# A two-layer decoder trunk: the first normalisation transposed ahead of its scale and offset

## The chip, the cores and the metric

The kernel runs on one core of one Trainium2 chip. The metric is device time in microseconds of one execution of the whole program; lower is better. TensorE (PE in the profile) multiplies and transposes, VectorE (DVE) and ScalarE (ACT) work on elements, GpSimd (POOL) does elementwise work and issues DMAs, SyncE (SP) issues DMAs.

## What is computed

Two post-norm layers on 256 tokens of 2048 channels. Each has a token mixer with cross-attention, an output projection, a first layer norm, a product-key expert retrieval (PEER) on the normalised tokens, and a second layer norm. What matters here, cut from the reference:

```python
def layer_norm(z, g, b):
    mu = jnp.mean(zf, axis=-1, keepdims=True)
    var = jnp.mean(jnp.square(zf - mu), axis=-1, keepdims=True)
    return (zf - mu) * lax.rsqrt(var + LN_EPS) * g + b

for i in range(DEPTH):                                   # 2 layers
    ...                                                  # mixer and cross-attention
    mix = jnp.concatenate([local, mem_out], axis=-1) @ w_o[i]
    x = layer_norm(DEEPNORM_ALPHA * x + mix, ln_g[i, 0], ln_b[i, 0])
    ffn = peer_ffn(x, peer_wq[i], peer_keys[i], peer_u[i], peer_v[i])
    x = layer_norm(DEEPNORM_ALPHA * x + ffn, ln_g[i, 1], ln_b[i, 1])
```

`peer_ffn` first multiplies x with `peer_wq` (2048 x 2048) for its queries.

## The kernel before

Tokens lie on partitions as two blocks of 128 (`c` = 0, 1) in `xres` (128 x 2 x 2048). Matmuls contract over channels, so each projection needs its input transposed: `xx` (tiles `xa` for channel blocks 0 to 7, `xb` for 8 to 15), with channels on partitions, each value as a `hi` and a `lo` part whose sum carries float32 precision. `split` (L102, L103) makes such a pair: ScalarE writes `hi`, VectorE subtracts it from the source for `lo`. Weights go the same way: `cut` loads 1 MB from DRAM into one of two `raw` buffers on SP's queue (L138), ScalarE makes `hi` and VectorE `lo` of it, 2048 wide, in two buffers each.

The first normalisation, `norm`, stands between the output projection (L171 to L173, whose results L849 adds to `xres`) and the query projection (`proj_t` with `peer_wq`, `mm_t` at L167 and L168). It takes the statistics (L229 to L235: `mv` the mean and variance, `rs` one over the deviation, `nm` minus mean times `rs`) and then goes through four chunks of 512 channels. In each chunk block 0 is normalised by two VectorE operations with the scale and offset rows of `gbt` (L254, L255), block 1 too in the first chunk; in the other three block 1 goes to ScalarE (L259) and GpSimd (L260 for the scale, L261 for the offset). `put_x` then transposes four 128 x 128 pieces of a block into one of two `tr` banks of PSUM (L271) and splits the bank into `xx`. Afterwards GpSimd's queue stores the normalised `xres` to `x1d` (L869), which is read back after the expert scan. `gbt` is `xres`-shaped data: 512 scales and 512 offsets, the same in every partition, loaded by GpSimd's queue (L249).

The first weight group of the query projection is two blocks of 256 columns. A block has two halves of 8 channel blocks, each one load of 1 MB; of each channel block TensorE makes two pairs of L167 (512 columns) and L168 (256 columns). So the first group has four weight halves: first and second for `xa`, third and fourth for `xb`. Behind the group come single blocks with the scores of the product keys (L443) between them; the `keys` tile is loaded on SP's queue (L422).

Each engine works through its own queue in a fixed order. The framework that builds the program sets that order when the program is built: it moves instructions by when it takes their inputs to be ready, so the order isn't that of the source text. Semaphores guard the dependencies, and an instruction that waits holds up all that stand behind it on its engine. `norm` stands twice in the program, once for each layer.

## Time and profile before

| what | us |
| --- | --- |
| median of 3 runs | 3461.08 (3458.07 to 3463.72) |
| profiled execution, its own time | 3457.87 |
| span of the profiled execution | 3456.1 |
| TensorE busy | 3323.3 |
| VectorE busy | 2433.7 |
| ScalarE busy | 1792.3 |
| GpSimd busy | 1317.7 |

The profile is of one execution. The table of engines says who is busy over the whole span; views of a stretch say who is in one place; a timeline lists one engine's instructions in order of time with the idle time before them and what ended it. An instruction is named by its line in the kernel, its operation, and the tiles it writes and reads.

### The profile page before, as it was taken

The page shows a single profiled execution, that of the slowest core. Times are in us where ns is not written, and L with a number is a line of the kernel's source. Part 1 is how long each engine was busy: PE and PEld are TensorE (multiplying, and loading weights), DVE is VectorE, ACT ScalarE, POOL GpSimd, SP SyncE. Part 2 cuts the span into 40 slices and gives each one's busy share as a digit, 9 for nine tenths or more (in the row PEclk, how much of TensorE's full clock was granted, in tenths as well). Part 3 has the DMA queues.
Part 4 walks back from the last instruction along what each step waited for, and adds up shares of the span by engine and source line. Part 5 has one row for each costly group of instructions (what it writes and reads, how often), then busy time and mean ns, then how long its engine had stood idle before and what let it go on. Part 6 is the DMA issues. An engine that isn't in the chain of part 4 may idle for free.

```text
span 3456.1 us, 48912 instructions
## 1 busy us (share of the span) xinstructions
PE 3323.3 (96%) x18444; PEld 2820.3 (82%) x18444; DVE 2433.7 (70%) x3842; ACT 1792.3 (52%) x2404; POOL 1317.7 (38%) x1008
## 2 busy tenths in 40 slices
PE   8998999999999799999999989999999999799997
PEld 7887888888888677877788878888888888688885
DVE  5657788677786477777755767786777785577777
ACT  4433445677744455555444433444777544455554
POOL 0001001587601268886000010001878301488885
PEclk9999999999999899999999999999999999899999
DMA  8454556558796688888554445555478777688885
GB/s 291 153 195 159 193 201 212 187 198 251 232 272 251 213 310 319 320 323 300 186 187 168 161 172 194 201 206 209 176 229 248 234 250 264 230 318 319 320 320 208
DMA packets 242320, 810.39 MB, mean 234 GB/s; under 512 B 120224, under 2 KB 120736, under 8 KB 173728
## 3 DMA queue, kind: packets, MB, share of 16 engines
q1 hardware_dynamic: 176160, 464.83, 40.7%
q0 software_dynamic: 65920, 342.41, 27.2%
q8 instruction: 145, 2.38, 0.3%
q14 instruction: 95, 0.78, 0.1%
HBM read 733.75 MB, written 73.40 MB: 234 GB/s over the span
## 4 chain that ended last, share of the span: by engine, by line
PE 39%; DVE 5%; issue 3%; DMA 2%; ACT 1%; POOL 0%; POOLq 0%; ACTq 0%; DVEq 0%
PE acc L167 13%; PE acc L168 7%; PE acc L172 4%; PE acc L173 4%; PE acc L171 3%; DVE lo L103 2%; DMA raw<-in_u_dram 1%; PE tr L172 1%; PE tr L173 1%; PE g L172 1%; PE g L173 1%; PE tr L171 1%; PE g L171 1%; ACT hi L102 1%; PE g L575 1%
## 5 line engine op out<-in xcount | busy, mean ns | idle before, releaser
L103 DVE TENSOR_TENSOR lo<-raw,hi 128x2048 fp32r<-128x2048 f32 (+1 forms) x520 | 1069.8, 2058 | 422.8 <-ACT hi L102 421.5
L102 ACT CAST hi<-raw 128x2048 fp32r<-128x2048 f32 (+1 forms) x520 | 895.3, 1722 | 452.0 <-PE acc L167 257.5
L167 PE MATMUL acc<-xa,hi 128*128 128x512 f32 x2656 | 958.2, 398 | 3.7 <-ACT hi L102 3.7
L167 PE MATMUL acc<-xb,hi 128*128 128x512 f32 x2656 | 935.4, 390 | 0.0
L168 PE MATMUL acc<-xa,lo 128*128 128x256 f32 x2656 | 758.5, 286 | 16.3 <-DVE lo L103 15.6
L168 PE MATMUL acc<-xb,lo 128*128 128x256 f32 x2656 | 750.6, 283 | 0.0
L167 PEld LDWEIGHTS acc<-xa,hi 128*128 128x128 f32 x2656 | 501.7, 189 | 102.9 <-ACT hi L102 4.4
L167 PEld LDWEIGHTS acc<-xb,hi 128*128 128x128 f32 x2656 | 498.7, 188 | 103.6
L694 POOL DMA_DIRECT2D agd<-am x256 | 143.3, 560 | 1066.5 <-ACT am L693 1043.4
L168 PEld LDWEIGHTS acc<-xa,lo 128*128 128x128 f32 x2656 | 504.7, 190 | 27.2 <-DVE lo L103 25.8
L168 PEld LDWEIGHTS acc<-xb,lo 128*128 128x128 f32 x2656 | 501.9, 189 | 0.7 <-DVE lo L103 0.3
L552 POOL TENSOR_SCALAR eq<-iota_n,nidx1T,sT 128x128 bf16<-128x128 bf16 x256 | 425.2, 1664 | 82.5 <-PE tr L577 76.4
L756 POOL DMA_INDIRECT ag<-agd,iw x226 | 352.3, 1559 | 86.0 <-issue 77.4
L103 DVE TENSOR_TENSOR lo<-vr,hi 128x2048 fp32r<-128x2048 f32 x114 | 261.1, 2290 | 79.8 <-ACT hi L102 78.7
L102 ACT CAST wh<-w 128x128 fp32r<-128x128 f32 (+1 forms) x226 | 78.9, 349 | 457.0 <-PE g L172 380.9
L693 ACT ACTIVATE am<-am 128x256 f32<-128x256 f32 x256 | 107.2, 419 | 389.4 <-DVE am L178 389.3
L557 DVE SCALAR_TENSOR_TENSOR pc<-iota_b,idx2T,gT 128x256 f16<-128x256 bf16 x512 | 221.6, 486 | 116.0 <-PE tr L577 116.0
L172 PE MATMUL acc<-lo,wh 128*128 128x512 f32 x664 | 268.2, 404 | 3.9 <-DVE lo L103 3.9
L173 PE MATMUL acc<-hi,wl 128*128 128x512 f32 x664 | 261.6, 394 | 1.7 <-DVE wl L103 1.7
L171 PE MATMUL acc<-hi,wh 128*128 128x512 f32 x664 | 208.4, 392 | 33.2 <-ACT wh L102 33.2
L743 POOL DMA_INDIRECT vr<-in_v_dram,iv x114 | 191.7, 1682 | 80.9 <-DVE lo L103 38.4
L102 ACT CAST hi<-vr 128x2048 fp32r<-128x2048 f32 x114 | 217.8, 1911 | 2.5 <-PE g L173 1.4
(258 smaller groups left out, 4745.9 us busy)
## 6 DMA issues: line engine op xcount, KB each, us to landing
raw<-in_u_dram SPq DMA_DIRECT2D x256, 1024.0 KB, 5.1
raw<-in_peer_wq_dram SPq DMA_DIRECT2D x32, 1024.0 KB, 4.8
agd<-am POOLq DMA_DIRECT2D x256, 128.0 KB, 4.5
raw<-in_w_in_b_dram SPq DMA_DIRECT2D x56, 512.0 KB, 4.0
agd<-gt SPq DMA_DIRECT2D x64, 320.0 KB, 7.8
rh<-in_w_in_a_dram SPq DMA_DIRECT2D x32, 512.0 KB, 4.3
rh<-in_w_o_dram SPq DMA_DIRECT2D x32, 512.0 KB, 3.7
raw<-in_w_o_dram SPq DMA_DIRECT2D x32, 512.0 KB, 4.1
```

The costliest lines, as they stand in the source:

```text
L102: nc.scalar.copy(hi, src)
L103: nc.vector.tensor_tensor(lo, src, hi.bitcast(F32), op=ALU.subtract)
L167: nc.tensor.matmul(o, wh, x1.rearrange("p n a t -> p (n a t)"), start=dc == 0, stop=False)
L168: nc.tensor.matmul(o[:, :T], wl, x1[:, 0, 0, :], start=False, stop=dc == ND - 1)
L171: nc.tensor.matmul(o, sh, mh, start=first, stop=False)
L172: nc.tensor.matmul(o, sh, ml, start=False, stop=False)
L173: nc.tensor.matmul(o, sl, mh, start=False, stop=last)
L552: nc.gpsimd.tensor_scalar(eq1[:, t, :], iota_n, n1, sc, op0=ALU.is_equal, op1=ALU.mult)
L557: nc.vector.scalar_tensor_tensor(pc[:, t], iota_b[:, None, :].to_broadcast([P, 2, NB]), idx["i2"][:, k:k + 1], idx["g"][:, k, :, None].to_ ...
L694: nc.gpsimd.dma_start(out=a3[:, b, :T], in_=am)
L743: nc.gpsimd.indirect_dma_start(out=vr, out_offset=None, in_=a[f"v{layer}"], in_offset=bass.IndirectOffsetOnAxis(ap=box["iv"][:, k:k + 1], ...
L756: nc.gpsimd.indirect_dma_start(out=ag, out_offset=None, in_=agd[:, :], in_offset=bass.IndirectOffsetOnAxis(ap=box["iw"][:, k:k + 1], axis=0))
```

## The change

`norm` is rewritten, and it gets the scales and offsets a second time in another layout: `gbT`, 128 x 32 values, with a channel in each partition (16 columns of scales, 16 of offsets), loaded by GpSimd's queue.

```diff
-    def norm(y, xo, stats, eps, gb, after):
+    def norm(y, stats, eps, gb, gbT, after):
         r = [ln_rstd(stats, c, eps) for c in range(NC)]
         xx = new_x()
         for ch in range(4):
-            gbt = gb(ch)
-            affine(y, xo, r[0], 0, ch, gbt, False)
-            affine(y, xo, r[1], 1, ch, gbt, ch != 0)
-            for c in range(NC):
-                put_x(xo, xx, c, ch)
+            f = slice(ch * 512, ch * 512 + 512)
+            nc.scalar.activation(y[:, 1, f], y[:, 1, f], AF.Identity, scale=r[1][1], bias=r[1][2])
+            nc.vector.tensor_scalar(y[:, 0, f], y[:, 0, f], r[0][0][:, 0:1], r[0][1], op0=ALU.subtract, op1=ALU.mult)
+            for h in range(2):
+                pt = tr_bank()
+                for j in range(2):
+                    dc = 4 * ch + 2 * h + j
+                    zt = pt[:, j * T:j * T + T]
+                    for c in range(NC):
+                        nc.tensor.transpose(zt[:, c * P:c * P + P], y[:, c, dc * P:dc * P + P], ident)
+                for j in range(2):
+                    dc = 4 * ch + 2 * h + j
+                    zt, x1 = pt[:, j * T:j * T + T], xx(dc)[:, 0]
+                    g, b = gbT[:, dc:dc + 1], gbT[:, ND + dc:ND + dc + 1]
+                    nc.scalar.activation(x1[:, 0, :], zt, AF.Identity, scale=g, bias=b)
+                    t = sm.tile([P, T], F32, name="xt", tag="cr", bufs=3)
+                    nc.vector.tensor_scalar(t, zt, g, b, op0=ALU.mult, op1=ALU.add)
+                    nc.vector.tensor_tensor(x1[:, 1, :], t, x1[:, 0, :].bitcast(F32), op=ALU.subtract)
             after(ch)
+        for ch in range(4):
+            f, gbt = slice(ch * 512, ch * 512 + 512), gb(ch)
+            for c, eng in ((1, nc.gpsimd), (0, nc.vector)):
+                eng.tensor_tensor(y[:, c, f], y[:, c, f], gbt[:, :512], op=ALU.mult)
+                eng.tensor_tensor(y[:, c, f], y[:, c, f], gbt[:, 512:], op=ALU.add)
         return xx
...
         gbl = [load_gb(lnp, 2 * layer, ch, 4) for ch in range(4)]
+        gbT = lnp.tile([P, 2 * ND], F32, name="gbT")
+        nc.gpsimd.dma_start(out=gbT, in_=a["ln_gbT"][layer])
...
-        xx = norm(xres, xres, stats, eps, gbl.__getitem__, after)
+        xx = norm(xres, stats, eps, gbl.__getitem__, gbT, after)
...
+        "ln_gbT": np.concatenate([z[:, 0].reshape(L, ND, P).transpose(0, 2, 1) for z in (ln_g, ln_b)], axis=2),
```

Now only mean and deviation are applied ahead of the transposition (L280 on ScalarE for block 1, L281 on VectorE for block 0). A `tr` bank takes half a chunk: two channel blocks with both token blocks (L288). Scale and offset, now one value for each partition, are applied on the way out of PSUM: by ScalarE into `hi` (L293), by VectorE into a float32 tile `xt` (L295), from which VectorE subtracts `hi` for `lo` (L296). `xres` in its natural layout gets scale and offset (L301, L302) in place, block 1 on GpSimd and block 0 on VectorE, once the chunk has been transposed; it is needed for the store to `x1d`. GpSimd does so for four chunks instead of three.

The build gives another order around `norm`; it is the same in both layers, and the rest of the program keeps its order but for some places in the key search just behind. On VectorE, from the statistics on, before:

```order
L103 TENSOR_TENSOR lo<-raw,hi 128x2048
L233 RECIPROCAL rs<-sd 128x1
L229 BN_AGGR mv<-stats 128x2
L254 SCALAR_TENSOR_TENSOR xres<-xres,mv,gbt 128x512
L235 SCALAR_TENSOR_TENSOR nm<-mv,rs 128x1
L233 RECIPROCAL rs<-sd 128x1
L255 SCALAR_TENSOR_TENSOR xres<-xres,rs,gbt 128x512
```

and in the changed kernel:

```order
L103 TENSOR_TENSOR lo<-raw,hi 128x2048
L233 RECIPROCAL rs<-sd 128x1
L229 BN_AGGR mv<-stats 128x2
L103 TENSOR_TENSOR lo<-raw,hi 128x2048
L235 SCALAR_TENSOR_TENSOR nm<-mv,rs 128x1
L233 RECIPROCAL rs<-sd 128x1
L281 TENSOR_SCALAR xres<-xres,mv,rs 128x512
L235 SCALAR_TENSOR_TENSOR nm<-mv,rs 128x1
L281 TENSOR_SCALAR xres<-xres,mv,rs 128x512 x3
L301 TENSOR_TENSOR xres<-xres,gbt 128x512
L295 TENSOR_SCALAR xt<-tr,gbT 128x256
```

The second weight half (`lo<-raw,hi`) has moved from behind the third chunk's L254 to the front, and the first L301 stands ahead of the first L295. Further on VectorE, up to the third and fourth weight halves, before:

```order
L254 SCALAR_TENSOR_TENSOR xres<-xres,mv,gbt 128x512
L103 TENSOR_TENSOR lo<-raw,hi 128x2048
L103 TENSOR_TENSOR xb<-tr,xb 128x4x128 x2
L255 SCALAR_TENSOR_TENSOR xres<-xres,rs,gbt 128x512
L103 TENSOR_TENSOR lo<-raw,hi 128x2048
L103 TENSOR_TENSOR xb<-tr,xb 128x4x128 x2
L103 TENSOR_TENSOR lo<-raw,hi 128x2048
```

and in the changed kernel:

```order
L301 TENSOR_TENSOR xres<-xres,gbt 128x512 x2
L295 TENSOR_SCALAR xt<-tr,gbT 128x256 x2
L296 TENSOR_TENSOR xb<-xt,xb 128x256 x2
L295 TENSOR_SCALAR xt<-tr,gbT 128x256
L302 TENSOR_TENSOR xres<-xres,gbt 128x512
L296 TENSOR_TENSOR xb<-xt,xb 128x256
L302 TENSOR_TENSOR xres<-xres,gbt 128x512
L301 TENSOR_TENSOR xres<-xres,gbt 128x512
L103 TENSOR_TENSOR lo<-raw,hi 128x2048
L302 TENSOR_TENSOR xres<-xres,gbt 128x512
L103 TENSOR_TENSOR lo<-raw,hi 128x2048
```

All sixteen L295 and L296 and seven of the eight L301 and L302 of block 0 now stand ahead of the third weight half. On TensorE, at the first transpositions and the first matmuls of the query projection (numbers tell buffers apart), before:

```order
L271 MATMUL tr_2222<-ident_72,xres_507 128x128 x4
L271 MATMUL tr_2229<-ident_72,xres_507 128x128 x4
L271 MATMUL tr_2241<-ident_72,xres_507 128x128 x4
L271 MATMUL tr_2248<-ident_72,xres_507 128x128 x4
L167 MATMUL acc_2332<-xa_2216,hi_2276 128x512
L168 MATMUL acc_2332<-xa_2216,lo_2277 128x256
L167 MATMUL acc_2333<-xa_2216,hi_2276 128x512
```

and in the changed kernel:

```order
L288 MATMUL tr_2222<-ident_72,xres_507 128x128 x3
L288 MATMUL tr_2235<-ident_72,xres_507 128x128 x3
L167 MATMUL acc_2387<-xa_2218,hi_2306 128x512
L168 MATMUL acc_2387<-xa_2218,lo_2307 128x256
L167 MATMUL acc_2388<-xa_2218,hi_2306 128x512
L168 MATMUL acc_2388<-xa_2218,lo_2307 128x256
L167 MATMUL acc_2389<-xa_2218,hi_2340 128x512
L288 MATMUL tr_2250<-ident_72,xres_507 128x128 x4
```

Where sixteen transpositions (two chunks) stood ahead of the first matmul, now eight do (one chunk, two halves), and the third half stands behind five matmuls, one of them of the second weight half. On SP's queue `keys` goes from behind the fourth load of `peer_wq` to behind the fifth, and waits for the last L302 of both engines.

## Rows read from the trace of the kernel before

**Rows 1.** The page's table of engines: busy us (share), instructions.

```profile
PE 3323.3 (96%) x18444; PEld 2820.3 (82%) x18444; DVE 2433.7 (70%) x3842; ACT 1792.3 (52%) x2404; POOL 1317.7 (38%) x1008
```

**Rows 2.** Stretches: us, busy PE, PEld, DVE, ACT, POOL; PE clock, DMA share, GB/s.

```profile
267.00:273.00 6.00, 0.06 (x2) 0.02 (x1) 5.98 (x14) 4.19 (x4) 0.00 (x0) 0.88 0.14 22
273.00:281.00 8.00, 4.23 (x17) 3.06 (x18) 7.85 (x9) 3.88 (x6) 6.91 (x5) 0.50 0.28 115
285.20:290.00 4.80, 4.80 (x32) 4.29 (x31) 2.80 (x4) 0.69 (x2) 0.55 (x1) 0.99 0.99 348
320.00:340.00 20.00, 16.69 (x97) 14.37 (x96) 19.97 (x56) 6.67 (x7) 0.00 (x0) 1.00 0.41 158
2058.50:2072.70 14.20, 10.20 (x44) 8.47 (x45) 14.05 (x16) 5.64 (x9) 9.82 (x7) 0.58 0.32 128
```

**Rows 3.** TensorE's timeline, layer 0: start, us, instruction [idle before <-who ended it].

```profile
272.98 1.12 PE L271 MATMUL tr<-ident,xres 128*128 128x128 f32 x4 [5.94 <-DVE xres L255]
276.05 1.11 PE L271 MATMUL tr<-ident,xres 128*128 128x128 f32 x4 [1.95 <-DVE xres L255]
...
281.62 0.63 PE L167 MATMUL acc<-xa,hi 128*128 128x512 f32 x1
282.05 0.41 PE L168 MATMUL acc<-xa,lo 128*128 128x256 f32 x1
...
295.85 0.39 PE L167 MATMUL acc<-xb,hi 128*128 128x512 f32 x1
...
306.94 1.67 PE L443 MATMUL tr<-keys,qT 128*128 128x128 f32 x12
```

**Rows 4.** VectorE's timeline, layer 0.

```profile
269.04 2.26 DVE L103 TENSOR_TENSOR lo<-raw,hi 128x2048 fp32r<-128x2048 f32 x1
271.22 0.16 DVE L233 RECIPROCAL rs<-sd 128x1 f32<-128x1 f32 x1
...
272.19 0.73 DVE L255 SCALAR_TENSOR_TENSOR xres<-xres,rs,gbt 128x512 f32<-128x512 f32 x1
...
274.24 3.44 DVE L255 SCALAR_TENSOR_TENSOR xres<-xres,rs,gbt 128x512 f32<-128x512 f32 x2
...
278.20 1.15 DVE L254 SCALAR_TENSOR_TENSOR xres<-xres,mv,gbt 128x512 f32<-128x512 f32 x1
279.27 0.68 DVE L103 TENSOR_TENSOR xa<-tr,xa 128x512 fp32r<-128x512 f32 x1
...
282.79 1.16 DVE L254 SCALAR_TENSOR_TENSOR xres<-xres,mv,gbt 128x512 f32<-128x512 f32 x1
...
291.49 2.29 DVE L103 TENSOR_TENSOR lo<-raw,hi 128x2048 fp32r<-128x2048 f32 x1 [3.49 <-ACT hi L102]
```

**Rows 5.** GpSimd's timeline, layer 0.

```profile
277.09 1.71 POOL L260 TENSOR_TENSOR xres<-xres,gbt 128x512 f32<-128x512 f32 x1
278.88 1.60 POOL L261 TENSOR_TENSOR xres<-xres,gbt 128x512 f32<-128x512 f32 x1
...
281.79 1.60 POOL L261 TENSOR_TENSOR xres<-xres,gbt 128x512 f32<-128x512 f32 x1
```

**Rows 6.** Groups by line and shape: busy us, mean ns of one | idle before.

```profile
L700 DVE TENSOR_TENSOR w<-ag 128x256 f32<-128x256 f32 x104 | 44.3, 426 | 27.1 <-DMA ag<-agd,iw 23.8
L406 DVE TENSOR_SCALAR sc<-sc,dw 128x256 f32<-128x256 f32 x12 | 3.5, 350 | 0.1
L406 DVE TENSOR_SCALAR sc<-sc,dw 128x128 f32<-128x128 f32 x12 | 2.7, 283 | 0.1
L589 DVE TENSOR_SCALAR m<-tr 128x256 f32<-128x256 f32 x2 | 0.8, 424 | 6.4 <-PE tr L577 6.4
L259 ACT ACTIVATE xres<-xres,nm,rs 128x512 f32<-128x512 f32 x8 | 6.3, 809 | 3.6 <-DVE nm L235 3.6
```

**Rows 7.** SP's queue, layer 0.

```profile
288.13 0.33 SPq L422 DMA_DIRECT2D keys<-in_keysT_dram  x1
293.81 46.78 SPq L138 DMA_DIRECT2D raw<-in_peer_wq_dram  x8
```

## The prediction

> **What bounds the kernel now.** I read the page's table of engines first: TensorE is busy 96% of the span [rows 1], so a change of a normalisation counts only by what TensorE idles or crawls around it. The two first normalisations (one in each layer) are such places. I then read the stretches of layer 0: TensorE does next to nothing from 267 to 273 us and is busy for 4.23 of the next 8 us, at a granted clock of 0.50 (1.2 GHz) after that pause; from 285.2 on it is busy all the time, at 0.99 (2.4 GHz) [rows 2]. TensorE's own timeline gives the marks [rows 3]: first four transpositions at 272.98 after 5.94 us idle, second half of the first weight group (first `xb` matmul) at 295.85, end of the group (the scores' first matmuls) at 306.94. Between the last two marks lie 32 pairs of L167 and L168: (306.94 - 295.85) / 32 = 0.347 us a pair.
>
> Who releases TensorE there is VectorE, busy for 5.98 of 6 us and 7.85 of 8 [rows 2]. Two things are to be seen in its timeline. First, the third weight half (`lo` at 291.49, done at 293.78) comes 2.1 us before TensorE wants it, after 3.49 us idle: VectorE has some 5 us of slack, no more. Second, L254 and L255 are slow beside GpSimd. GpSimd's op of 277.09 ends at 278.80, and the L254 issued at 278.20 ends 0.55 later; GpSimd's op of 281.79 ends at 283.39, and the L254 issued at 282.79 ends 0.56 later; the two L255 of 274.24 take 3.44 together, against 0.73 for the one of 272.19 ahead of GpSimd's first op [rows 4, 5]. So a VectorE operation with two SBUF tensors waits out a GpSimd operation and then runs. The `lo` part of `put_x`, with one tensor in PSUM, keeps its 0.68 in the middle of the GpSimd op of 278.88 [rows 4, 5].
>
> **The change, term by term, for one layer.** The ten L254/L255 and eight 512-wide `xa`/`xb` subtractions go from VectorE. It gets 4 L281, 16 L295, 16 L296 and 8 L301/L302, and in the order seven of those last eight stand ahead of the third weight half.
>
> Start. The second weight half (as the first: 2.26 long, the next start 2.18 after its own [rows 4]) now stands ahead of `nm`, so the first L281 starts near 273.8, where the first L254 followed the first half directly. L281 512 wide: a TENSOR_SCALAR costs 283 ns at 128 and 350 at 256 [rows 6], 67 per 128 elements, so an estimate of 0.48. ScalarE's L280 for the other token block takes 0.81 (L259 [rows 6]) from 274.4, and the eight transpositions of the first chunk end near 276.75 at 0.26 each (1.11 and 1.12 for four, with the last one's latency, at the low clock [rows 3]). Before, the second four ended at 277.2, so this is no loss. But VectorE's next instruction is an L301 that overwrites what is being transposed; it waits, about 1.2 us.
>
> VectorE's work to the third `lo`. L295 reads PSUM: 424 ns, as L589 [rows 6], 0.34 to the next start (0.08 overlaps, as 2.26 against 2.18 above). L296: 426 as L700 [rows 6], 0.34 too. L301/L302: 0.68, 0.61 to the next start. 16 x 0.34 + 16 x 0.34 + 7 x 0.61 + 2.2 for the `lo` = 17.4. From 276.75 that ends at 294.1, even if nothing waits: the same place as before, and all the slack is used.
>
> GpSimd's lock. L296, L301 and L302 have two SBUF tensors each; 23 of them meet 8 GpSimd operations instead of six. Before, the four blocked ones shown lost 3.44 - 1.46 = 2.0 and twice 0.45, or 2.9 us [rows 4]. No row shows a TENSOR_TENSOR with both tensors in SBUF beside a GpSimd operation. Its bounds are the unblocked `xa` subtraction (0) and the blocked L255 (1.0 each). I take the blocked end, since the operands are alike. A GpSimd op runs 1.1 to 1.2 us of its own (that of 278.88 took 1.60, of which it waited for the L254 until 279.35), and VectorE's pairs L296, L296 fall into each: laid beside each other, five are blocked for the whole op (1.15) and three for 0.45 to 0.8, together 7.6 us.
>
> TensorE's order. Only two `tr` banks exist and a bank now holds half a chunk. The third half's transpositions stand behind five matmuls of the first two channel blocks, which wait for L296 of these; L295 of the third half waits for them in turn. At the low clock the next start comes 0.43 after a L167's (281.62 to 282.05 [rows 3]) and half of that after a L168's: 3 x 0.43 + 2 x 0.21 + 4 x 0.26 = 2.75, of which VectorE covers 0.85 with two L296 and a L295 of its own. That makes 1.9 once, and a few tenths at the four later halves: 2.6.
>
> So the third `lo` ends at 294.1 + 7.6 + 2.6 = 304.3, and TensorE, which wanted it at 295.85, gets it 8.5 late. With the short waits at the second one I take **9 us**. ScalarE is no bound: 16 L293 of 0.4 and 4 L280 lie in VectorE's shadow; if it were to wait, each of its waits is one of VectorE's.
>
> Weight loads behind. Two `raw` buffers: a load is issued when an earlier `lo` is done (293.81 against the end at 293.78 [rows 4, 7]). The fifth load moves from 293.8 to 304.4. `keys` on SP's queue now waits for the last L302 and GpSimd's last op, so it is issued at about 305 instead of 288.13 [rows 7], with the sixth load behind it on the queue, and the second store to `x1d`, later on GpSimd's queue because eight ops stand ahead, at 305 too. Four transfers of 1 MB then start within 3 us; at the 348 GB/s of the stretch 285.2 to 290 [rows 2] they need 12 us. So the sixth load lands near 319, its `lo` ends near 323.5 and frees the buffer for the eighth, which lands near 329, where TensorE needs it already cut; the wait there is about 5.7. In before TensorE idles 20 - 16.69 = 3.3 us between 320 and 340 [rows 2], part of which it replaces. Net **3 us**, with 0 and 5 as bounds. The scores wait for `keys` at about 316, inside the same loss. The store is read back only after the expert scan, and `gbT`, 16 KB, is loaded ahead of the last projection block: both cost nothing.
>
> Sum for one layer: 9 + 3 = 12. Layer 1 has the same order and the same picture (14.2 us with 10.20 busy at a clock of 0.58 [rows 2]), so 24. The stages behind are bound by TensorE and carry the delay to the end. The profiled execution took 3457.87, 1.8 over its span, and so 3481.9 after; the median of the three runs stands 3.2 higher, so **3485 us**, 0.7% slower.
>
> In the Trainium skill, the page "SBUF — State Buffer", section "Who interferes with whom", says that a VectorE instruction with two SBUF inputs, `tensor_tensor` included, contends with a GpSimd instruction that reads SBUF, and that the later one blocks fully. The L254 rows agree for their kind of instruction; no row here shows it for a TENSOR_TENSOR. By that rule the lock term is the 7.6 above; if it did not hold for this kind, the term is nought and the sum is the second rival's.
>
> **Rivals.**
> 1. *The start gets shorter and wins.* Transposed values need no scale rows, and per-partition scalars are cheap; TensorE lost 5.94 + (8 - 4.23) = 9.7 us to gaps before 281 [rows 2, 3]. If neither lock nor TensorE's order made VectorE wait, and L295/L296 went at half their rows, 5.4 us less would bring the third `lo` to 288.7, and TensorE, full from 285 now, could be so from about 281.5: 3.5 us a layer, 3485 - 24 - 7 = 3454. It decides from the point at which the third `lo` ends before 295.85. Against it: 17.4 us of work have 19.1 to lie in. Chance 0.05.
> 2. *TENSOR_TENSOR is not blocked by GpSimd.* Then 7.6 falls away, the third `lo` ends at 296.7, 1 to 2 us late with the wait at the fourth, and the bunched loads keep their 3: 5 a layer, 3471. Chance 0.13.
> 3. *Off the path.* The group's later weights have slack enough and TensorE's old idle of 3.3 us at 320 to 340 swallows the delay: 3461 within 0.2%. Against it: 3.3 is less than 9. Chance 0.05.
> 4. *The clock stays at 1.2 GHz longer*, since matmuls now come in short bursts until 300. A pair at that level costs some 0.64 from start to start (0.43 + 0.21 as above) against 0.347; ten more such pairs are 3 us a layer: 3491. Chance 0.10.
>
> **How the numbers follow.** The forecast has 0.67. All but rivals 1 and 3 are slower by more than 0.2% (6.9 us, about what a measurement here can tell from none): 0.90; same 0.05, faster 0.05. The range takes in the bounds of the lock (3471, less 1) and of the clock (3491, plus 1): 3470 to 3492.
>
> **What would show it.** Right: in both layers the third `lo` ends near 304, L296 rows split into 0.42 and 1.2 to 1.6, TensorE's first `xb` pairs come 8 us later and a wait of 4 to 6 us for `lo` stands near 330. Wrong: L296 at 0.42 throughout beside GpSimd (rival 2), first `xb` pairs by 296 (rivals 1, 3), clock under 0.7 to 295 (rival 4). The forecast falls if transpositions of the third half start before 279, since then VectorE is fed early.

## The result: 3484 us, 0.7% slower

The changed kernel took 3484.4 us (median of 4 runs, 3481.9 to 3485.3) beside 3460.6 for the kernel before: a ratio of 1.0066, interval 1.0054 to 1.0079. Five more runs of it beside another set of runs of before (below) gave 3481.4, a ratio of 1.0062, 1.0049 to 1.0076. So it is slower, by 21 to 24 us, where 24 were forecast.

The profile after, read in the order of the prediction. First the table of engines (busy us, share, instructions), which answers to [rows 1]:

```profile
PE 3335.5 (96%) x18444; PEld 2827.8 (81%) x18444; DVE 2454.6 (70%) x3894; ACT 1801.4 (52%) x2422; POOL 1279.9 (37%) x1014
```

The stretches (us, busy PE, PEld, DVE, ACT, POOL; PE clock, DMA share, GB/s), against [rows 2]:

```profile
273.00:281.00 8.00, 2.71 (x9) 1.93 (x10) 7.10 (x14) 4.29 (x7) 3.08 (x2) 0.50 0.60 246
285.20:290.00 4.80, 3.94 (x25) 3.37 (x24) 3.86 (x7) 1.66 (x4) 2.64 (x2) 0.94 0.00 0
304.00:310.00 6.00, 5.81 (x19) 5.04 (x20) 2.94 (x3) 0.00 (x0) 0.55 (x1) 0.52 0.79 239
320.00:340.00 20.00, 17.48 (x93) 15.04 (x92) 20.00 (x84) 5.05 (x6) 0.00 (x0) 0.91 0.46 160
```

TensorE is now idle for 0.86 of the 4.80 us from 285.2 on, where it was full, and no DMA runs there: both `raw` buffers are taken, since no `lo` frees one. From 304 on TensorE runs at half its clock once more, and the transfers that had stood still come together.

TensorE's timeline (start, us, instruction, [idle before <- who ended it]), the marks of [rows 3]:

```profile
274.37 0.69 PE L288 MATMUL tr<-ident,xres 128*128 128x128 f32 x2 [7.27 <-DVE xres L281]
275.29 1.54 PE L288 MATMUL tr<-ident,xres 128*128 128x128 f32 x6 [0.23 <-ACT xres L280]
...
301.10 0.74 PE L167 MATMUL acc<-xb,hi 128*128 128x512 f32 x2 [1.45 <-ACT hi L102]
304.19 0.80 PE L168 MATMUL acc<-xb,lo 128*128 128x256 f32 x2 [2.35 <-DVE lo L103]
...
317.00 2.12 PE L461 MATMUL tr<-keys,qT 128*128 128x128 f32 x16
333.20 0.50 PE L168 MATMUL acc<-xa,lo 128*128 128x256 f32 x2 [2.52 <-DVE lo L103]
```

The first L168 on `xb` stands at 304.19, against 296.08 before: 8.1 late. The first scores stand at 317.00, against 306.94: 10.1 late. From TensorE's timeline before come the first row behind, and the two waits that it had between 320 and 340:

```profile
296.08 0.28 PE L168 MATMUL acc<-xb,lo 128*128 128x256 f32 x1
...
322.27 0.71 PE L443 MATMUL tr<-keys,qT 128*128 128x128 f32 x4 [1.64 <-DVE qT L178]
...
324.66 0.50 PE L168 MATMUL acc<-xa,lo 128*128 128x256 f32 x2 [1.68 <-DVE lo L103]
```

VectorE's timeline and below it GpSimd's, against [rows 4, 5]:

```profile
276.65 0.69 DVE L301 TENSOR_TENSOR xres<-xres,gbt 128x512 f32<-128x512 f32 x1 [0.90 <-PE tr L288]
...
287.18 2.04 DVE L296 TENSOR_TENSOR xa<-xt,xa 128x256 fp32r<-128x256 f32 x2
...
294.50 0.75 DVE L296 TENSOR_TENSOR xb<-xt,xb 128x256 fp32r<-128x256 f32 x2
295.17 1.28 DVE L301 TENSOR_TENSOR xres<-xres,gbt 128x512 f32<-128x512 f32 x2
...
301.85 2.28 DVE L103 TENSOR_TENSOR lo<-raw,hi 128x2048 fp32r<-128x2048 f32 x1
```

```profile
287.58 1.35 POOL L302 TENSOR_TENSOR xres<-xres,gbt 128x512 f32<-128x512 f32 x1
...
295.04 2.57 POOL L301 TENSOR_TENSOR xres<-xres,gbt 128x512 f32<-128x512 f32 x1 [1.65 <-ACT hi L102]
...
299.35 0.59 POOL L889 DMA_DIRECT2D x1d<-xres  x1 [0.30 <-POOL xres L302]
305.03 0.55 POOL L889 DMA_DIRECT2D x1d<-xres  x1 [5.08 <-DVE xres L302]
```

A pair of L296 takes 0.75 where GpSimd is idle, and 2.04 where GpSimd's op of 287.58 starts 0.40 behind it: the first gets through, the second waits out the op. At 295 it is the other way round: GpSimd's op of 295.04 comes while the L296 pair of 294.50 runs and takes 2.57, and VectorE's two L301, which follow that pair at once, run through it at 0.64 each. The third `lo` ends at 304.13.

ScalarE and VectorE at the third half chunk, and further on at the weight half that TensorE waits for near 333:

```profile
283.46 0.56 ACT L293 ACTIVATE xa<-tr,gbT 128x256 fp32r<-128x256 f32 x1 [1.53 <-PE tr L288]
284.06 0.55 DVE L295 TENSOR_SCALAR xt<-tr,gbT 128x256 f32<-128x256 f32 x1 [1.55 <-ACT xa L293]
284.64 0.56 ACT L293 ACTIVATE xa<-tr,gbT 128x256 fp32r<-128x256 f32 x1 [0.62 <-DVE xt L295]
...
324.59 1.92 ACT L102 CAST hi<-raw 128x2048 fp32r<-128x2048 f32 x1 [3.90 <-PE acc L167]
330.87 2.28 DVE L103 TENSOR_TENSOR lo<-raw,hi 128x2048 fp32r<-128x2048 f32 x1
```

L295 reads the bank and not `hi`, and yet it starts only when L293 has ended, and the next L293 when L295 has: in this program the two engines take turns at a bank.

The groups by shape (busy us, mean ns of one | idle before):

```profile
L295 DVE TENSOR_SCALAR xt<-tr,gbT 128x256 f32<-128x256 f32 x32 | 16.4, 537 | 4.3 <-ACT xa L293 4.3
L296 DVE TENSOR_TENSOR xb<-xt,xb 128x256 fp32r<-128x256 f32 x16 | 11.2, 732 | 0.0
L296 DVE TENSOR_TENSOR xa<-xt,xa 128x256 fp32r<-128x256 f32 x16 | 10.8, 708 | 0.0
L302 DVE TENSOR_TENSOR xres<-xres,gbt 128x512 f32<-128x512 f32 x8 | 6.7, 834 | 0.0
```

### The profile page after: what moved, and what is told of

Its sections match the earlier page's. It is cut to its first block, busy times and chain, and to the rows that moved or that the text cites. A ratio compares the mean times of both kernels' runs of the same rounds, so it can differ in the third digit from the quotient of the medians.

```text
span 3483.4 us, 49017 instructions
## 1 busy us (share of the span) xinstructions
PE 3335.5 (96%) x18444; PEld 2827.8 (81%) x18444; DVE 2454.6 (70%) x3894; ACT 1801.4 (52%) x2422; POOL 1279.9 (37%) x1014
## 3 DMA queue, kind: packets, MB, share of 16 engines
q0 software_dynamic: 65984, 342.44, 27.3%
## 4 chain that ended last, share of the span: by engine, by line
PE 39%; DVE 6%; issue 3%; DMA 2%; ACT 1%; POOL 0%; POOLq 0%; ACTq 0%; DVEq 0%
PE acc L167 13%; PE acc L168 7%; PE acc L172 4%; PE acc L173 4%; PE acc L171 3%; DVE lo L103 2%; PE tr L172 1%; PE tr L173 1%; PE g L172 1%; PE g L173 1%; PE tr L171 1%; PE g L171 1%; DMA raw<-in_u_dram 1%; ACT hi L102 1%; PE g L593 1%
## 5 line engine op out<-in xcount | busy, mean ns | idle before, releaser
L167 PE MATMUL acc<-xa,hi 128*128 128x512 f32 x2656 | 965.5, 401 | 10.5 <-DVE xa L296 3.7
L167 PE MATMUL acc<-xb,hi 128*128 128x512 f32 x2656 | 939.4, 392 | 2.9 <-ACT hi L102 2.9
L168 PE MATMUL acc<-xa,lo 128*128 128x256 f32 x2656 | 761.8, 287 | 15.3 <-DVE lo L103 14.3
L168 PE MATMUL acc<-xb,lo 128*128 128x256 f32 x2656 | 752.2, 284 | 4.7 <-DVE lo L103 4.7
L167 PEld LDWEIGHTS acc<-xa,hi 128*128 128x128 f32 x2656 | 505.0, 190 | 111.4 <-issue 8.2
L167 PEld LDWEIGHTS acc<-xb,hi 128*128 128x128 f32 x2656 | 500.6, 189 | 107.8 <-ACT hi L102 3.8
L168 PEld LDWEIGHTS acc<-xa,lo 128*128 128x128 f32 x2656 | 508.3, 192 | 27.2 <-DVE lo L103 25.7
L168 PEld LDWEIGHTS acc<-xb,lo 128*128 128x128 f32 x2656 | 504.1, 190 | 6.4 <-DVE lo L103 5.9
L570 POOL TENSOR_SCALAR eq<-iota_n,nidx1T,sT 128x128 bf16<-128x128 bf16 x256 | 416.4, 1630 | 83.5 <-PE tr L595 77.1
L172 PE MATMUL acc<-lo,wh 128*128 128x512 f32 x664 | 268.0, 404 | 4.6 <-DVE lo L103 4.6
L761 POOL DMA_INDIRECT raw<-in_v_dram,iv x112 | 158.5, 1415 | 119.6 <-DVE lo L103 80.8
```

Source lines behind the costliest of these rows:

```text
L167: nc.tensor.matmul(o, wh, x1.rearrange("p n a t -> p (n a t)"), start=dc == 0, stop=False)
L168: nc.tensor.matmul(o[:, :T], wl, x1[:, 0, 0, :], start=False, stop=dc == ND - 1)
L172: nc.tensor.matmul(o, sh, ml, start=False, stop=False)
L570: nc.gpsimd.tensor_scalar(eq1[:, t, :], iota_n, n1, sc, op0=ALU.is_equal, op1=ALU.mult)
L761: nc.gpsimd.indirect_dma_start(out=vr, out_offset=None, in_=a[f"v{layer}"], in_offset=bass.IndirectOffsetOnAxis(ap=box["iv"][:, k:k + 1], ...
```

## The experiments

The forecast's theory was weighed against three others throughout. It says: VectorE's queue ahead of the third weight half sets the time, with GpSimd's lock in it, and the late `lo` bunches the transfers behind. The others: the lock costs nothing (rival 2), or TensorE's new order of half chunks does it, or the loss isn't about the place ahead of the third half at all.

A table sums up where each kernel stood against the kernel before, by the start of the same instruction in each trace: the first scores of layer 0 (306.94 before), the L172 that waits for `lo` at 1417.68 before, in the stage of the expert values, the first scores of layer 1 (2092.42), and the span's end (3456.1). All in us of delay.

| kernel | scores 0 | 1417.68 | scores 1 | end | median us |
| --- | --- | --- | --- | --- | --- |
| changed kernel | 10.1 | 8.2 | 23.9 | 27.3 | 3484.4 |
| the same, second trace | 10.0 | 10.8 | 20.3 | 21.0 | 3481.4 |
| e1, no GpSimd ops | 3.7 | 5.9 | 10.4 | 15.6 | 3472.4 |
| e2, no VectorE L301/L302 | 4.9 | 8.0 | 11.7 | 11.8 | 3468.3 |
| e3, neither | -0.3 | 1.4 | 1.5 | 4.1 | 3461.9 |
| e4, `xt` on ScalarE | 3.7 | 10.2 | 15.0 | 23.2 | 3482.7 |
| e5, stores held | 9.5 | 7.7 | 18.9 | 19.9 | 3478.3 |
| e6, `keys` early | 9.1 | 13.4 | 25.3 | 29.7 | 3484.8 |
| e7, stores held, no GpSimd ops | 1.7 | 2.5 | 7.2 | 7.9 | 3465.8 |
| e8, moved behind the group | 2.4 | 12.8 | 12.1 | 25.2 | 3482.8 |
| e10, unlocked split | 8.0 | 5.6 | 14.0 | 12.4 | 3470.0 |
| e11, unlocked, stores held | 2.9 | -0.5 | 3.7 | 2.1 | 3459.9 |
| e12, kernel before, stores held | -0.6 | 2.9 | 2.9 | 5.8 | 3460.5 |

The last row shows how far one trace can be trusted: e12 is as fast as the kernel before by its median, and yet its trace is 5.8 late at the end. The stage itself begins at slightly different times too, from 1.3 us earlier (e3) to 1.2 later (e8) than before by the first L229, and that is in the first column. Differences of one or two microseconds in the first column, and of some 3 to 6 in the others, show nothing by themselves; the medians decide.

### Without GpSimd's operations, without VectorE's, without either (e1, e2, e3)

e1's edit; e2 keeps `(1, nc.gpsimd)` alone, and e3 drops the loop (L298 to L302).

```diff
-            for c, eng in ((1, nc.gpsimd), (0, nc.vector)):
+            for c, eng in ((0, nc.vector),):
```

> The scale and offset of the stored copy are left out for token block 1 (the eight GpSimd operations of each layer), so the stored copy of that block is not finished; VectorE's instructions around the normalisation stay the same, in the same order. The forecast's theory: VectorE loses only the time in which it is locked out. In the changed kernel the blocked L296 and the blocked L302 lost 0.62 + 1.07 + 1.29 + 1.25 + 1.31 = 5.5 us in layer 0 against their free 0.75 a pair and 0.65, so all L296 should now show about 0.42, the third `lo` should start at 301.85 - 5.5 = 296.3 and end at 298.6, and with 1 to 1.5 us less from the loads behind it (`keys` and the second store no longer wait for GpSimd) a layer should gain some 6.5 to 7: 3484.4 - 13.5 = 3471 (3467 to 3475). Rival 'the lock hardly matters, it is VectorE's plain work and TensorE's order': 3481 to 3485, with the third `lo` still ending at 303 or later.

Measured: 3472.4 us, ratio to before 1.0031 (1.0021 to 1.0041), 9 to 12 us under the changed kernel's two medians. Its groups (busy us, mean ns of one | idle before), and its third `lo` from VectorE's timeline:

```profile
L296 DVE TENSOR_TENSOR xb<-xt,xb 128x256 fp32r<-128x256 f32 x16 | 6.2, 417 | 0.0
L296 DVE TENSOR_TENSOR xa<-xt,xa 128x256 fp32r<-128x256 f32 x16 | 6.2, 417 | 0.0
L302 DVE TENSOR_TENSOR xres<-xres,gbt 128x512 f32<-128x512 f32 x8 | 5.5, 682 | 0.0
```

```profile
296.60 2.28 DVE L103 TENSOR_TENSOR lo<-raw,hi 128x2048 fp32r<-128x2048 f32 x1
```

VectorE's instructions and their order around the normalisation are the same in both kernels, so the difference of the means is the lock: 16 x (720 - 417) + 4 x (834 - 682) ns = 5.46 us a layer (720 is the mean of 708 and 732). The third `lo` agrees: it ends 22.01 us behind the start of the first L301 (298.88 against 276.87), 27.48 in the changed kernel (304.13 against 276.65), 5.47 less. Rival 2 falls: a TENSOR_TENSOR with both tensors in SBUF is blocked by GpSimd. The 9 to 12 us aren't the lock alone, since the store of block 1 went out earlier too; e7 below sets that right.

> The scale and offset of the stored copy are left out for token block 0 (the eight L301/L302 of VectorE in each layer); GpSimd's eight stay. The order moves: the third `lo` goes ahead of the last two chunks' L295 and L296. The forecast's theory (VectorE's whole queue ahead of the third `lo` sets the time): VectorE loses 4 x (0.68 - 0.07) + 4 x (0.83 - 0.07) = 5.5 us of work with what lock is in it, and the 0.9 us wait of the first L301 for the transpositions; the L296 that are blocked stay blocked. 6.4 a layer, and with the third `lo` ahead of the last chunks 1 to 2 us more from the weight loads: 3484.4 - 2 x 8 = 3468 (3464 to 3473). Rival 'only the lock costs': the lock of the four blocked pairs of L296 (4.9 of 5.5 us) remains, so at most 0.6 a layer: 3483. Rival 'two token blocks' natural copies cost nothing, TensorE's order of half chunks does': 3482 or more.

Measured: 3468.3, ratio 1.0019 (1.0009 to 1.0028). The gain of 13 to 16 us is about what the forecast's theory gave for VectorE's queue (16), and far more than the lock's share in it. VectorE's work is not all of it, though: the third `lo` now stands ahead of the last three L295 (and is itself held up by GpSimd, 3.38 instead of 2.28), and the store of block 0 leaves at 276.59 instead of 305.03, ahead of the bunch. The two rows are from VectorE's and GpSimd's timelines:

```profile
293.53 3.38 DVE L103 TENSOR_TENSOR lo<-raw,hi 128x2048 fp32r<-128x2048 f32 x1
...
276.59 0.54 POOL L889 DMA_DIRECT2D x1d<-xres  x1 [84.21 <-DVE xres L281]
```

> Scale and offset of the stored copy are left out for both token blocks (GpSimd's eight and VectorE's eight operations of each layer, and the loads of their rows). What stays of the change: the half chunks on TensorE, L293, L295 and L296. The forecast's theory: the two removals add, 5.5 of lock and 5.5 + 0.9 of work make 12 us, more than the 9 that TensorE waits in a layer, so the third `lo` ends near 292, TensorE's group ends where it did before (306.9) and the whole goes back to 3460 (3455 to 3465). Rival 'the order of half chunks and the per-partition operations on the way out of PSUM (L295 at 0.54, L296) cost the most': it stays at 3470 or more, with waits of TensorE for `xt` and L296 ahead of the third half. Rival 1 of the prediction (the start gets shorter): 3454 or less.

Measured: 3461.9, ratio 0.9996 (0.9987 to 1.0006). No loss is left that the runs can tell from none, and nothing is gained. The first scores, from TensorE's timeline:

```profile
306.64 1.57 PE L456 MATMUL tr<-keys,qT 128*128 128x128 f32 x12 [0.21 <-DMA keys<-in_keysT_dram]
```

They stand at 306.64, against 306.94 before, in a trace whose stage began 1.3 earlier: a microsecond longer. So the half chunks, L293, L295 and L296 cost about what L254, L255 and `put_x` cost, and nearly the whole loss comes from scale and offset "on the side", with what they do to the stores (which leave at 274.73 and 277.23 here, ahead of the bunch). The gains of e1 and e2, 9 to 12 and 13 to 16, are together as much as the 20 to 23 of e3 or more. Rival 1 falls too: a shorter start isn't there even when the side work costs nothing.

### `xt` on ScalarE (e4)

```diff
-                    nc.scalar.activation(x1[:, 0, :], zt, AF.Identity, scale=g, bias=b)
-                    nc.vector.tensor_scalar(t, zt, g, b, op0=ALU.mult, op1=ALU.add)
+                    nc.scalar.activation(t, zt, AF.Identity, scale=g, bias=b)
+                    nc.scalar.copy(x1[:, 0, :], t)
```

> The whole computation, with another share of it: ScalarE writes `xt` out of PSUM with scale and offset and then copies it to `hi`; VectorE keeps only the subtraction L296. VectorE loses 16 x (0.54 - 0.08) = 7.4 us, ScalarE gets sixteen more operations: 16 x (0.56 + 0.4) + 4 x 0.8 for block 1 + 2 x 1.9 for the weights = 22 us of the 30 us from 274.4 to 304. The forecast's theory (VectorE's queue ahead of the third `lo` is the bound): the third `lo` 6 to 7 us earlier, about as much as the lock allows, and 3484.4 - 2 x 7 = 3470 (3466 to 3476). Rival 'ScalarE, or the longer chain bank, xt, hi, lo, takes the place of VectorE': the group's end moves by 4 us or less, the bunched loads behind it keep their loss, 3480 to 3486.

Measured: 3482.7, ratio 1.0071 (1.0054 to 1.0088): no gain to be measured, and the rival's number, though not for its reason. The first step came in part as the forecast's theory has it: the third `lo` ended at 299.78, 4.4 us earlier than in the changed kernel (6 to 7 were expected), and the first scores came 6.4 earlier. At 1417.68 it was 10.2 late again. Where the gain went is seen in ScalarE's, VectorE's and TensorE's timelines behind the group:

```profile
310.72 1.90 ACT L102 CAST hi<-raw 128x2048 fp32r<-128x2048 f32 x1 [5.11 <-DMA raw<-in_peer_wq_dram]
...
312.65 2.29 DVE L103 TENSOR_TENSOR lo<-raw,hi 128x2048 fp32r<-128x2048 f32 x1 [6.54 <-ACT hi L102]
314.86 0.42 DVE L178 TENSOR_TENSOR qT<-acc,cr 128x256 f32<-128x256 f32 x1
...
315.34 1.65 PE L461 MATMUL tr<-keys,qT 128*128 128x128 f32 x6 [3.92 <-DVE qT L178]
```

Both stores, `keys` and two weight loads are issued from 296.65 on; the fifth weight load, issued at 299.81, is awaited by ScalarE until 310.7. VectorE's `lo` for it waits 6.54 us, the sum for `qT` stands behind it on VectorE's queue, and TensorE's scores wait for that. So the bunch of transfers is a loss of its own.

### The stores, `keys`, and the lock with the stores alike (e5, e6, e7)

e5 holds both stores by adding zero times a column of query block 9 to one column of `xres` ahead of each. e6 gives `keys` a pool of its own (the second diff). e7 is e5 with e1's edit.

```diff
+                z = sm.tile([P, 1], F32, name="z", tag="rs")
+                nc.vector.tensor_scalar_mul(z, qT[:, 9, 0:1], 0.0)
+                for c in range(NC):
+                    nc.gpsimd.tensor_tensor(xres[:, c, 0:1], xres[:, c, 0:1], z, op=ALU.add)
+                    nc.gpsimd.dma_start(out=x1d[c], in_=xres[:, c])
```

```diff
+        kp = right.enter_context(tc.tile_pool(name=f"kp{layer}", bufs=1, side="right"))
...
-        keys = pk.tile([P, 16, P], F32, name="keys")
+        keys = kp.tile([P, 16, P], F32, name="keys")
```

> The whole computation; the two stores to `x1d` are held back until query block 9 (some 340 us): zero times one of its columns is added to one column of `xres` by GpSimd ahead of each store. Around the normalisation nothing else changes. The forecast's theory (its second term): at 304 to 307 us the fifth and sixth weight load, `keys` and the second store start together; without the store three transfers remain, some 3 us less of traffic, the wait of TensorE near 330 shrinks from some 5 us by 2 to 3, and a layer gains 2 to 3: 3484.4 - 5 = 3479 (3476 to 3482). Rival 'the store takes nothing from the loads, only the third `lo` counts': 3484 within 2. Rival 'the bunched transfers are the larger half of the loss': 3474 or less.

Measured: 3478.3, ratio 1.0053 (1.0036 to 1.0069): 3 to 6 us less than the changed kernel's two medians, as the forecast's theory expected in sum, but the intervals overlap, so a gain isn't shown by this run. The place was another, too. The wait for `lo` near 330 went from 2.52 only to 2.17, and the first scores moved by 0.5.

> The whole computation; `keys` gets a pool of its own, whose place in SBUF nothing else uses before it, so that its load no longer waits for the last L302 and stands far ahead on SP's queue. Like the run with the held stores it takes one of four transfers from the bunch at 304 to 307 us, and the sixth weight load no longer stands behind it on the queue. The forecast's theory: a layer gains 1 to 3, 3480 (3477 to 3483); the third `lo` stays at 302. Rival 'the wait near 330 is not for loads': 3484 within 2.

Measured: 3484.8, ratio 1.0071 (1.0053 to 1.0089): nothing gained, the rival's number. Taking `keys` out of the bunch is worth nothing by itself: its trace was ahead by 1 us at the first scores and behind at 1417.68. TensorE's waits near 330 are 1.63 and 1.68 here, as in the kernel before. The prediction had counted `keys` among the causes of its second term.

> As the run with the held stores, and in addition the scale and offset of the stored copy are left out for token block 1 (GpSimd's eight operations of each layer). In the run without GpSimd's operations one of the stores had also moved away from the weight loads, so its gain of 12 us was lock and loads together; here both sides hold their stores alike, and the difference to the run with the held stores is the lock alone. The lock as read from VectorE's rows (5.3 us at the third `lo`: 304.13 against 298.88): 10 to 11 us below that run, 3468 (3465 to 3472). Rival 'the lock's 5.3 us are given back behind the group': within 4 us of it.

Measured: 3465.8, ratio 1.0015 (1.0005 to 1.0024), 12.5 us under e5, with stores alike in both: the lock, 5.46 us a layer by VectorE's rows, comes through to the end with a little more.

### Scale and offset behind the first weight group (e8)

The loop of L298 to L302 and the two stores become a function, called where the first weight group ends; the rows come from the pool of the key search.

```diff
+        gbl = [load_gb(pk, 2 * layer, ch, 4) for ch in range(4)]
...
+            if state["nb"] == 0:
+                natural(xres, gbl.__getitem__, x1d)
```

> The whole computation; the scale and offset of the stored copy (on both engines) and the stores stand behind the first weight group in the program, about 305 us, and their rows are loaded into the pool of the key search. Nothing of it is ahead of the third `lo` any more. Theory 'place': the loss comes from standing ahead of the third and fourth weight half; the group then ends where it did in the run without these operations (306.6), and the whole lands at 3461 to 3467. Rival 'VectorE has no slack behind the group either' (it is busy 19.97 of 20 us from 320 to 340 before the change, 20.00 after): 5.5 us of work and the lock of GpSimd's operations with the 2.2 us `lo` subtractions come back as waits behind 306: 3473 to 3482.

Measured: 3482.8, ratio 1.0064 (1.0047 to 1.0081): just above the rival's range. The first scores were only 2.4 late, in a trace whose stage began 1.2 late, but at 1417.68 it was 12.8. VectorE's and TensorE's rows behind the group:

```profile
309.49 0.69 DVE L304 TENSOR_TENSOR xres<-xres,gbt 128x512 f32<-128x512 f32 x1 [3.43 <-DMA gbt<-in_ln_gb_dram]
...
313.56 3.11 DVE L305 TENSOR_TENSOR xres<-xres,gbt 128x512 f32<-128x512 f32 x2
...
321.85 1.58 DVE L305 TENSOR_TENSOR xres<-xres,gbt 128x512 f32<-128x512 f32 x1
...
328.53 2.29 DVE L103 TENSOR_TENSOR lo<-raw,hi 128x2048 fp32r<-128x2048 f32 x1
...
330.87 0.80 PE L168 MATMUL acc<-xb,lo 128*128 128x256 f32 x2 [5.23 <-DVE lo L103]
```

The same operations, blocked by GpSimd's again (1.4 to 1.8 us each), push the key search back; the `lo` of 328.53 stands behind the key search on VectorE's queue, and TensorE waits 5.2 us for it. The run isn't a clean one, though: the rows are now loaded at this place (2 MB), VectorE waits 3.4 us for the first of them, and they share the DMA with the weights. So it shows that this way of moving the work behind the group gains nothing; how much of the 12.8 is the work and how much the loads stays open.

### The split without two SBUF tensors, and with the stores held (e9, e10, e11, e12)

e9 is the changed kernel once more. e11 is e10 with e5's held stores, and e12 the kernel before with held stores. e10 leaves all work where it is and takes away only what makes L296 wait: the value stays in PSUM.

```diff
-                    nc.vector.tensor_scalar(t, zt, g, b, op0=ALU.mult, op1=ALU.add)
-                    nc.vector.tensor_tensor(x1[:, 1, :], t, x1[:, 0, :].bitcast(F32), op=ALU.subtract)
+                    nc.vector.scalar_tensor_tensor(zt, zt, g, x1[:, 0, :].bitcast(F32), op0=ALU.mult, op1=ALU.subtract)
+                    nc.vector.tensor_scalar(x1[:, 1, :], zt, b, None, op0=ALU.add)
```

> The changed kernel once more, unaltered, for a second trace beside the held stores. In its first trace layer 0 lost 10.1 us up to the first scores, had 8.2 left at 1426 us and then lost 6.6 more in the stage of the expert values (GpSimd's indirect loads of 1532 to 1546 us took 2.4 to 2.8 us to issue instead of 0.95); with the held stores the same stage lost 0.5. If that is chance of one execution, the second trace has 0 to 2 there, a span near 3478, and the median of more rounds comes down to 3479 to 3483. If the early stores cause it, the second trace loses 5 to 7 there again and the median stays at 3484.

Measured: 3481.4 (3478.9 to 3482.4), span 3477.1. In this trace the stage of the expert values lost nothing (10.8 late at 1417.68, 10.8 still at the last statistics of layer 1), so the 6.6 us of the first trace are no property of the change. What made them is open: indirect loads that take over 2 us to issue stand in both traces. The changed kernel's own loss in this trace is 21.0, 10.8 and 10.2 in the two layers.

> The whole computation, written so that VectorE's part of the split has no operation with two SBUF tensors: in place in the PSUM bank it takes scale times the value minus `hi`, and a second operation adds the offset on the way from the bank to `lo`. GpSimd keeps its eight operations, VectorE its eight L301/L302. Forecast's theory (L296 loses 4.9 us a layer to GpSimd's lock): the lock of L296 goes; the second operation now reads PSUM, some 0.1 longer, 1.6 in all; 3.3 us a layer or more are gained, 3477 (3471 to 3480), and no operation of the split shows more than 0.6. Rival 'the bank is held longer, so transpositions wait and eat the gain': 3482 to 3486.

Measured: 3470.0, ratio 1.0033 (1.0023 to 1.0044), 11 to 14 us under the changed kernel, more than expected. The two new operations, with GpSimd as busy beside them as ever:

```profile
L294 DVE SCALAR_TENSOR_TENSOR tr<-tr,gbT,xb 128x256 f32<-128x256 f32 x16 | 7.2, 482 | 0.0
L295 DVE TENSOR_SCALAR xb<-tr,gbT 128x256 fp32r<-128x256 f32 x16 | 7.1, 475 | 0.1
```

```profile
314.96 1.19 PE L460 MATMUL tr<-keys,qT 128*128 128x128 f32 x4 [6.31 <-DMA keys<-in_keysT_dram]
```

The first fence holds groups (mean ns behind the comma), the second is of TensorE's timeline. Neither operation is ever blocked (the longest take 486 and 484 ns). Both together take 0.96 us, against 0.537 + 0.720 = 1.26 for L295 and L296: 16 x 0.30 = 4.8 us a layer. The expectation had 3.3, the lock of L296 less 1.6 for a longer read of PSUM; the second operation is indeed 0.06 longer than a free L296, but the first is 0.055 shorter than L295. The first L168 on `xb` stands at 296.68, 0.6 late instead of 8.1; the order had moved too, the third `lo` (294.35) now stands ahead of the last chunk's operations, and how much of the 11 to 14 that gives isn't shown. What is left is the row of the second fence: TensorE waits 6.3 us for `keys`.

> Both edits, the split without two SBUF tensors and the two stores held until query block 9; the whole computation. If lock and stores are two separate losses, their gains add: 3477 less the 6 that holding gave, 3471 (3463 to 3474), still not below the kernel before (3461), since VectorE's work is longer than before. If both gains are of the same wait, it stays at 3475 to 3478.

Measured: 3459.9, ratio 0.9995 (0.9986 to 1.0005): level with the kernel before, and below both ranges that were expected. The two gains add, 11 to 14 and 10.1, and each is larger than expected. Holding the stores is worth 10 us here, clear of the noise, and 3 to 6 in e5, not clear of it. The DMA view of 300 to 316 us (issues: line, engine, operation, count, KB each, median us to landing) shows why, e10's row first, then e11's:

```profile
keys<-in_keysT_dram SPq DMA_DIRECT2D x1, 1024.0 KB, 9.7
```

```profile
keys<-in_keysT_dram SPq DMA_DIRECT2D x1, 1024.0 KB, 4.9
```

In e10 `keys` is issued at 305.11, right behind the two stores of 303.27 and 304.81, and lands 9.7 us later; in e11 it is issued at 304.81 and lands 4.9 later, and TensorE's wait for it is 1.46 us instead of 6.31.

> A control: the kernel before the change with its two stores held until query block 9, nothing else; the whole computation. If holding the stores only undoes the bunch of transfers that the change makes, it is worth nothing here: 3460, within 4 either way. If it is a gain of its own, whatever the normalisation, it shows here too: 3450 to 3455, and the equality of the unlocked kernel with held stores then hides a remaining loss of the change of 5 to 10 us.

Measured: 3460.5, ratio 1.0001 (0.9992 to 1.0010). Held stores are worth nothing where nothing bunches: what e11 gained by them is loss that the change had made.

No version beat the kernel before. e3 shows why none that keeps this way through the transposition was to be expected: even with the side work left out it takes as long as the old one.

## Why the prediction was right, point by point

The sum came out (3485 forecast, 3484.4 and 3481.4 measured), and so did the first mark: the third `lo` ends at 304.13 in the trace, 304.3 was forecast. The mechanism, VectorE's queue with the lock in it ahead of the third weight half, is the one that the runs show. That the numbers came so close is partly luck: the terms were off in both directions.

- **Start.** The first L301 starts at 276.65 (276.75 forecast) after waiting 0.90 us for the transpositions (1.2). Right.
- **VectorE's plain work to the third `lo`, 17.4 us.** Too small. In e1, where no lock is, the stretch takes 298.88 - 276.87 = 22.0 us, of which 1.46 + 0.69 are waits that ScalarE's L293 ended: 19.9 of work. The largest miss is L295, priced as L589 at 424 ns; it takes 537, and 16 x 0.11 = 1.8 us.
- **GpSimd's lock, 7.6 us.** Right in kind, too large: 5.46. Five whole blocks of 1.15 and three smaller ones had been counted. The rows show four L296 blocked by 1.1 to 1.3, one L302 by 0.6, and one meeting, that of 295.04, in which GpSimd came second and lost its time instead.
- **TensorE's order, 2.6 us, with ScalarE at nothing.** VectorE's waits there are 1.46 + 0.69 = 2.15 us in e1 and 1.55 + 0.94 = 2.49 in the changed kernel. The size is right, the reason only half: in each wait the last 0.6 us are ScalarE's L293, which has to end before L295 starts (rows of 283.46 and 284.06), so that some 1.3 of the 2.49 are late transpositions. The prediction had L295 wait for the bank alone, took L293 for 0.4 (it takes 0.56) and called ScalarE no bound.
- The sum of the three, with plain work and waits as in e1, is 19.9 + 5.5 + 2.1 = 27.5, the measured 304.13 - 276.65, where 17.4 + 7.6 + 2.6 = 27.6 had been forecast. The mark was hit because one term was 2.5 too small and another 2.1 too large.
- **9 us at TensorE.** 8.1 at the first L168 on `xb`, 10.1 at the first scores. The other 2 are the clock: at 304 to 310 it is granted at 0.52, half speed, after the waits of 1.45 and 2.35 us with two matmuls ahead of them and two between. Busy 5.81 us at that clock, TensorE does 5.81 x 0.48 = 2.8 us less work; 0.7 of it had been done ahead of the wait (four L167 on `xb` instead of one, 0.23 from start to start). The fourth rival had the mechanism, but ahead of 300, where the clock stands at 0.94 to 1.00. That TensorE would fall back to 1.2 GHz behind the wait the prediction did not have.
- **Weight loads behind, 3 us (0 to 5).** The step whose reason was wrong. TensorE's wait near 330 was forecast at 5.7, for the eighth load. It is 2.52, against 1.64 + 1.68 = 3.3 before, it is for the seventh half, and it is not for a load: that half's `lo` starts at 330.87, directly behind an instruction of the key search on VectorE's queue, while its `hi` had been done at 324.59 + 1.92 = 326.5. The eighth half isn't wanted before 339.96. What the place costs more than before is the clock behind the wait: at 0.91 over 320 to 340 TensorE does 17.48 x 0.09 = 1.6 us less work, so 2.5 + 1.6 - 3.3 = 0.8. From the first scores to the end of the layer the second trace lost 0.7 us, and the first had regained 1.9 by 1417.68; both are within what e12's trace drifts. That the transfers bunch is true, and e4 and e10 show that it costs 5 to 7 us a layer once the third `lo` comes earlier. That in the changed kernel most of this lies in the shadow of the first term is argued and not shown.
- **Layer 1** repeats layer 0: 10.8 and 10.2 us in the second trace, where 12 each were forecast. That the first set of runs came within 1 us of 3485 may owe something to the 6.6 us that its trace lost elsewhere (e9).

The Trainium skill's page "SBUF — State Buffer", section "Who interferes with whom", had been set against the second rival. Its rule for a `tensor_tensor` with two SBUF inputs holds here: 417 ns without GpSimd, 720 in the mean beside it. So does its converse on that page of the Trainium skill, that a VectorE instruction with at most one SBUF input outside the two-port modes does not contend with GpSimd: the two operations of e10 keep their 482 and 475 ns.

## What to carry to other kernels

Work put "to the side" is free only if its engine has slack in the stretch where it now lies and locks no engine that has none: here VectorE had some 5 us of slack, got the eight operations of the stored copy and a lock of 5.5 us, and TensorE paid for what was over. Where VectorE has to work beside GpSimd, try to keep one operand in PSUM: the kernel written so (e10) gave back 11 to 14 of 21 to 24 us, some 10 of it by VectorE's rows, the rest with a changed order. And when a wait is taken away, look at what has piled up behind it: the stores and `keys` that start together cost another 10 us once the first wait was gone.

## What the runs showed of the hardware that was not expected

- A TENSOR_SCALAR from PSUM with two per-partition operands, 128 x 256, takes 537 ns (542 in e1, without GpSimd); the subtraction in place in PSUM takes 482, and adding one per-partition offset from PSUM 475. L589, by which it had been priced, has 424 [rows 6].
- Who is blocked depends on who comes second: GpSimd's L301 of 295.04, which came in the middle of an L296 pair, took 2.57 us, twice the 1.29 to 1.37 of its neighbours, while the two L301 of VectorE that followed the pair took 1.28 together.
- In the kernel before, two waits of 1.64 and 1.68 us near 322 and 324 left TensorE's clock at 1.00 [rows 2]; in the changed kernel 320 to 340, with one wait of 2.52, has a mean of 0.91: behind that wait an L167 and the L168 after it take 0.64 us from start to start (334.11 to 334.75), against 0.35 ahead of it.
